# Sparse-attention encoder step: memory-branch pieces tied to a softmax, a weight pair split on ScalarE, values' low halves on VectorE

## The chip, the cores and the metric

The kernel runs on one core of one Trainium2 chip. The metric is the device time of one execution in microseconds, the median of the runs; lower is better. The engines are named as in the profile: PE is TensorE (matmuls; PEld its weight loads), DVE is VectorE, ACT is ScalarE, POOL is GpSimd, and SP is the engine that issues the transfers (DMAs).

## The reference

One layer of a streaming encoder on 1024 prompt tokens and 64 sample tokens, width 1024. Three branches of the normalised input are mixed by sigmoid gates:

```python
def dsa_attend(qa, qi, wi, qpos, ka, va, ki, topk):          # branch a
    s = jax.nn.relu(jnp.einsum('bthd,bsd->bths', qi, ki))
    score = jnp.einsum('bths,bth->bts', s, wi)               # indexer
    ...
    _, sel = lax.top_k(score, topk)
    ...
    logits = jnp.einsum('bthgd,btjhd->bthgj', q, k_sel) * (HD_A ** -0.5)
    probs = jax.nn.softmax(logits, axis=-1)
    return jnp.einsum('bthgj,btjhd->bthgd', probs, v_sel)

def merge_and_ffn(x, a, b, m, gates, w_oa, w_ob, w_om, w_out, g_ffn, w_gate, w_up, w_down):
    ga, gb, gm = jnp.split(jax.nn.sigmoid(gates), N_BRANCH, axis=-1)
    mixed = ga * (a @ w_oa) + gb * (b @ w_ob) + gm * (m @ w_om)
    x = x + mixed @ w_out
    h = rmsnorm(x, g_ffn)
    return x + (jax.nn.silu(h @ w_gate) * (h @ w_up)) @ w_down
```

Branch a has 8 query heads on 2 key heads of 64; b is a pooling mixer; m is attention into 256 memory tokens. The kernel does not gather the chosen keys: it adds a score that holds a large penalty for keys that were not chosen.

## The kernel before

Everything is one function, `encoder_step`, on one core. Float32 products are made of float32r halves: a value is rounded to a high half, the rest is its low half, and `matmul3` multiplies high by high, low by high and high by low. So each weight block of 128x1024 costs a DMA into `raw`, a rounding `whi` (`round_hi`: POOL, or ACT where `third[0]` says so, line 95) and a subtraction `wlo` on DVE (`lo_of`, line 87). `whi` and `wlo` are rings of two buffers, so a rounding waits until the matmuls of the block two before it are done.

The Tile framework places the instructions: it reorders what is written by its own timeline, so the order on an engine is not that of the source. Each engine then runs its own list in order and waits on semaphores. `tc.issue_after(x)` makes the instructions under it that run on the engine of x stand behind x in that engine's list.

The stage in question is the attention of branch a, 668 to 868 us of the profile. The tokens are nine blocks (b = 0 to 7 of 128 prompt tokens, 8 the sample's 64), walked in the order 2, 7, 1, 6, 0, 8, 5, 4, 3; block b has 128(b+1) keys. Around this stage the steps are:

- `fill_gate`: sigmoid gates (a tanh, `fsg`, on ACT, line 244), stored through DMAs to `side_a`; the last one runs at the stage's start. The loads of values (`vf`) and queries (`q`) follow on SP.
- `split_values`: high halves of all values (`vb`) on ACT (L947), low halves on POOL (L948), eight of each.
- `queries_t(b)`: loads q, splits it (`split_queries`: high on ACT, L803, low on POOL, L804), transposes it on PE into `qT`.
- `softmax(b, kv)`: for four heads, logits on PE (L985, into the `tr` banks), score added and a minimum taken on DVE (as the maximum of the negated logits; "maximum" below) (`pr`, `mx`, L995, one pass), exponential on ACT (L997); then a reciprocal on DVE (L999) and four normalisations on POOL (L1001).
- `values(b, kv)`: by 128 keys, four transposes of `pr` on PE (L1014), split on ACT (`ph`, L1017) and DVE (`pl`, L87), and two matmuls into `acc` (L1021); at the end a sum of the two halves (`ot` or `a_held`, L1025 to 1029). It runs one step behind its softmax.
- `halves_of` and `release`: branch a's result is split into `bh` (ACT, L1038) and `bl` (POOL or, for the last block, DVE, L1039). These replace branch m's, so the results of six blocks are held in `a_held` until the fills that read the old content are done.
- `fill_om(f, ci)`: a piece of the memory branch (row block f of eight, one of three column pieces `OCH`): 12 matmuls on PE (L123) into the single bank `fl`, a multiply with the gate on DVE (L639), an addition on POOL (L640), a DMA to `side_a` (L641). There are 24 such fills. They are PE work that depends on nothing in the attention, and they use 8 weight pairs: four for the first two column pieces, and four again for the third. "First", "second", "third", "fourth" pair mean these in order.
- `merge`: the same for branch a with `w_oa`; four of the merges are written right after the attention (`f` 0 to 3, first column piece, into `tr` banks) and read only blocks 0 to 2, which are released early. After them comes the row stage with the remaining merges (its first matmul here: L123 `mm`, 128x352).

The main loop runs softmax(b, kv), one fill (or two, late), then values of the step before.

Of the kernel before, what the change touches and what calls it, by code (L numbers as in the profile page):

```python
# [46 lines left out]
def encoder_step(ctx: ExitStack, tc: tile.TileContext, a: dict, o: list):  # L47
# [581 lines left out]

    def fill_om(f, ci, other=False):  # L630
        if (f // 2, ci == 2) not in om_w:
            om_w[f // 2, ci == 2] = wblock(a["w_om"][f:f + 2].rearrange("f p k j -> p f k j"), (2, 4, 128))
        ow = om_w[f // 2, ci == 2]
        c0, cn = OCH[ci]
        c1 = c0 + cn
        gt, pin = merge_bufs(side_m, f, c0, c1)
        ps = mm()[:, :cn] if other else fps(cn)
        matmul3(ps, [(ow[0][:, f % 2, k], ow[1][:, f % 2, k], bh[:, k, c0:c1], bl[:, k, c0:c1]) for k in range(4)])
        V.scalar_tensor_tensor(gt, gt, 1.0, ps, op0=OP.add, op1=OP.mult)  # L639
        G.tensor_tensor(pin, pin, gt, op=OP.add)  # L640
        SP.dma_start(side_a[f, 1, :, c0:c1], pin)  # L641
# [160 lines left out]
    def split_queries(qs, q, n, eng=V):  # L802
        A.copy(qs[:n, :, 0], q[:n])  # L803
        eng.tensor_tensor(qs[:n, :, 1], q[:n], qs[:n, :, 0].bitcast(F32), op=OP.subtract)  # L804
# [126 lines left out]
    HELD = (0, 1, 2, 6, 7, 8)  # L931
    a_held = []
    with tc.tile_pool(name="att", bufs=1, side="right") as ap_:
# [9 lines left out]
        def split_values():  # L943
            for b0, b1, n in ((0, 4, 128), (4, 8, 128), (8, 9, 128), (9, 10, 64)):
                for kv in range(2):
                    vs = vf[b0 // 8][:n, b0 % 8:b0 % 8 + b1 - b0, kv * HDA:(kv + 1) * HDA]
                    A.copy(vb[:n, b0:b1, kv, 0], vs)  # L947
                    G.tensor_tensor(vb[:n, b0:b1, kv, 1], vs, vb[:n, b0:b1, kv, 0].bitcast(F32), op=OP.subtract)  # L948

# [19 lines left out]
        def softmax(b, kv, qT):  # L969
            n, nk, k0 = TS[b][1], nkey[b], 0 if b < 8 else SEQ  # L970
            if True:
                probs = []
                sm = ap_.tile([128, 4], F32, name="sm", tag="sm", bufs=4)[:n]
                for g in ORDER:
# [20 lines left out]
                    V.tensor_tensor_reduce(as_view(pr, nk), bank_view(lg, nk)[:n], as_view(score[b][:n], nk),  # L995
                                           scale=1.0, scalar=3.4e38, op0=OP.add, op1=OP.min, accum_out=mx)
                    A.activation(pr, pr, AF.Exp, bias=mx, scale=-1.0, accum_out=sm[:, len(probs):len(probs) + 1])  # L997
# [6 lines left out]
        def values(b, kv, probs):  # L1004
# [3 lines left out]
            if True:  # L1008
                acc = psum[0].tile([128, 512], F32, name="acc", tag="acc", bufs=1)[:, :4 * n]
                nj = len(blocks)  # L1010
                for ji, (c, cn, vi) in enumerate(blocks):
                    pt = mm() if rest or ji % 3 != 2 else fps(512)
                    for i in range(4):
                        PE.transpose(pt[:cn, i * n:(i + 1) * n], probs[i][:, c:c + cn], ident[:n, :n])  # L1014
# [2 lines left out]
                    A.copy(ph, pt[:cn, :4 * n])  # L1017
                    lo_of(pl, pt[:cn, :4 * n], ph)
                    vv = vb[:cn, vi, kv].rearrange("p s d -> p (s d)")
                    for i, r in enumerate((ph, pl)):  # L1020
                        PE.matmul(acc, vv, r, start=ji == 0 and i == 0, stop=ji == nj - 1 and i == 1)  # L1021
# [15 lines left out]
        def halves_of(av, cs, t0, n, eng):  # L1037
            A.copy(aoh[:, cs, t0:t0 + n], av)  # L1038
            eng.tensor_tensor(aol[:, cs, t0:t0 + n], av, aoh[:, cs, t0:t0 + n].bitcast(F32), op=OP.subtract)  # L1039
# [10 lines left out]
        for b in BLOCKS:  # L1050
            qT = queries_t(b)
            for kv in range(2):
# [7 lines left out]
                for _ in range(1 if b in HELD else late_fills.pop(0)):  # L1060
                    fill_om(*rest.pop(0))
                if todo:
                    values(*todo)
# [4 lines left out]
        values(*todo)
        release(HELD[3:])

    def merge(f, c0, cn, gt, pin, ps):
# [4 lines left out]
        matmul3(ps, [(ow[0][:, f % 2, k], ow[1][:, f % 2, k], aoh[:, k, c0:c1], aol[:, k, c0:c1]) for k in range(4)])
        V.scalar_tensor_tensor(gt, gt, 1.0, ps, op0=OP.add, op1=OP.mult)
        V.tensor_tensor(pin, pin, gt, op=OP.add)

    oa_w, early_pin = {}, []  # L1080
    FIRST = [(f, 0) for f in range(0, KT, 2)]
    for f in range(4):
        gt, pin = merge_bufs(side_a, f, 0, ACH[0][1])
        merge(f, *ACH[0], gt, pin, tr()[:, :ACH[0][1]])
        early_pin.append(pin)
# [539 lines left out]
```

## Time and profile before

| | us |
|---|---|
| median of 3 runs (1716.28 to 1719.61) | 1718.47 |
| the profiled execution | 1719.66 |
| its span in the profile | 1717.9 |
| PE busy | 1687.7 (98%) |
| DVE busy | 1146.7 (67%) |
| ACT busy | 808.1 (47%) |
| POOL busy | 408.8 (24%) |

The mean granted TensorE clock is 0.996. Three quarters of the chain of work that ended last is in the matmuls of other stages; the stage 668 to 868 us is read by stretches. A stretch row has start and end, its length, the busy time of each engine with its number of instructions, the clock granted to TensorE, the share of the DMA engines and GB/s. In timeline rows the first number is the start, the second the duration; in brackets stands how long the engine was idle before and what ended that.

### The profile page before, as it was taken

What the parts mean: (1) busy time and instruction counts of PE and PEld (TensorE: products, weight loads), DVE (VectorE), ACT (ScalarE), POOL (GpSimd) and SP (SyncE); (2) the same over time, 40 slices, a digit from 0 to 9 for tenths busy, and PEclk for the clock granted to TensorE, in tenths of its full rate; (3) what the DMA queues carried; (4) which work ended last, traced back from release to release, by engine and by line L of the source; (5) the groups of instructions that cost most, each with busy time, mean ns of one, the idle gap of its engine ahead of it and who ended that gap; (6) DMA issues with size and microseconds to landing.
All of it is one profiled execution on the core that took longest, in us unless ns stands there. A gap on an engine that the chain in (4) does not pass through costs nothing.

```text
span 1717.9 us, 32353 instructions
## 1 busy us (share of the span) xinstructions
PE 1687.7 (98%) x11992; PEld 1639.2 (95%) x11992; DVE 1146.7 (67%) x2558; ACT 808.1 (47%) x1943; POOL 408.8 (24%) x479
## 2 busy tenths in 40 slices
PE   8999999999999998999999999999999999999999
PEld 7999999999999998997798999999999999999999
DVE  7566999999974342787773678557667666465543
ACT  5456677746633442568632443333334333353331
POOL 4200425355421122675303431001101000000000
PEclk9999999999999999999999999999999999999999
DMA  6121541223466325452176536443535443497661
GB/s 231 49 70 56 174 146 48 71 89 110 129 201 201 102 86 181 159 177 78 51 274 214 198 114 236 144 144 125 203 114 187 145 169 102 160 361 230 216 191 53
DMA packets 150654, 257.13 MB, mean 150 GB/s; under 512 B 17240, under 2 KB 95696, under 8 KB 150496
## 3 DMA queue, kind: packets, MB, share of 16 engines
q1 hardware_dynamic: 150496, 255.07, 45.4%
q8 instruction: 94, 1.54, 0.4%
q14 instruction: 64, 0.52, 0.1%
HBM read 175.73 MB, written 79.29 MB: 148 GB/s over the span
## 4 chain that ended last, share of the span: by engine, by line
PE 62%; DVE 4%; DMA 3%; issue 2%; ACT 1%; POOL 1%; SPq 0%; DVEq 0%; ACTq 0%; POOLq 0%
PE mm L1279 24%; PE mm L1506 12%; PE mm L123 11%; PE fl L123 8%; PE acc L1021 1%; PE tr L985 1%; DMA side_m<-fpt 1%; PE mm L1014 1%; DVE lo L87 1%; PE tr L123 0%; DMA raw<-s 0%; PE mm L674 0%; DVE pl L87 0%; DVE wlo L87 0%; DVE pr L995 0%
## 5 line engine op out<-in xcount | busy, mean ns | idle before, releaser
L1279 PE MATMUL mm<-hi,whi 128*128 128x288 f32 (+1 forms) x1120 | 323.1, 289 | 2.3 <-ACT whi L1271 2.3
L1279 PE MATMUL mm<-hi,wlo 128*128 128x288 f32 (+1 forms) x1120 | 323.7, 290 | 1.2 <-DVE wlo L87 1.0
L1279 PE MATMUL mm<-lo,whi 128*128 128x288 f32 (+1 forms) x1120 | 323.5, 289 | 0.0
L1279 PEld LDWEIGHTS mm<-hi,whi 128*128 128x128 f32 x1120 | 211.9, 189 | 3.0 <-ACT whi L1271 3.0
L1279 PEld LDWEIGHTS mm<-hi,wlo 128*128 128x128 f32 x1120 | 211.0, 189 | 1.7 <-DVE wlo L87 1.6
L1279 PEld LDWEIGHTS mm<-lo,whi 128*128 128x128 f32 x1120 | 211.8, 189 | 0.0
L123 PE MATMUL fl<-hh,whi 128*128 128x362 f32 (+1 forms) x576 | 190.0, 330 | 0.4 <-ACT hh L135 0.4
L123 PE MATMUL fl<-hl,whi 128*128 128x362 f32 (+1 forms) x576 | 189.7, 330 | 0.1
L123 PE MATMUL fl<-hh,wlo 128*128 128x362 f32 (+1 forms) x576 | 188.1, 330 | 0.0
L1506 PE MATMUL mm<-ul,wh 128*128 128x256 f32 (+1 forms) x600 | 171.7, 288 | 0.0
L1506 PE MATMUL mm<-uh,wh 128*128 128x256 f32 (+1 forms) x600 | 171.4, 289 | 0.1
L1506 PE MATMUL mm<-uh,wl 128*128 128x256 f32 (+1 forms) x600 | 170.4, 288 | 0.0
L854 ACT ACTIVATE junk_a<-score,cand_a,sgn_a 128x512 f16<-128x512 f32 (+2 forms) x93 | 95.5, 1027 | 42.4 <-DVE cand_a L871 30.8
L1506 PEld LDWEIGHTS mm<-uh,wh 128*128 128x128 f32 x600 | 112.5, 188 | 0.5 <-ACT wh L1496 0.3
L1506 PEld LDWEIGHTS mm<-ul,wh 128*128 128x128 f32 x600 | 112.8, 188 | 0.0
L1506 PEld LDWEIGHTS mm<-uh,wl 128*128 128x128 f32 x600 | 112.3, 188 | 0.0
L123 PEld LDWEIGHTS fl<-hh,whi 128*128 128x128 f32 x576 | 108.2, 188 | 1.7 <-ACT hh L135 0.6
L123 PEld LDWEIGHTS fl<-hl,whi 128*128 128x128 f32 x576 | 108.3, 188 | 0.9 <-DVE hl L87 0.4
L123 PEld LDWEIGHTS fl<-hh,wlo 128*128 128x128 f32 x576 | 108.0, 188 | 0.6
L87 DVE TENSOR_TENSOR wlo<-raw,whi 128x512 fp32r<-128x512 f32 (+1 forms) x64 | 66.1, 1047 | 61.6 <-ACT whi L1271 37.9
L87 DVE TENSOR_TENSOR wl<-raw,wh 128x512 fp32r<-128x512 f32 x75 | 51.7, 689 | 70.2 <-ACT wh L1496 70.2
L857 DVE TENSOR_SCALAR_CACHE_REDUCE junk_v<-score,cand_v 64x192 f16<-64x192 f32 (+1 forms) x124 | 93.9, 757 | 2.6
(431 smaller groups left out, 4597.1 us busy)
## 6 DMA issues: line engine op xcount, KB each, us to landing
uf<-u SPq DMA_DIRECT2D x75, 272.0 KB, 4.4
raw<-in_w_up_dram SPq DMA_DIRECT2D x26, 512.0 KB, 4.5
fraw<-in_w_gates_dram SPq DMA_DIRECT2D x23, 512.0 KB, 3.7
fr<-in_w_gate_dram SPq DMA_DIRECT2D x22, 512.0 KB, 3.7
dr<-in_w_down_dram SPq DMA_DIRECT2D x22, 512.0 KB, 5.7
s<-dr SPq DMA_DIRECT2D x22, 512.0 KB, 3.0
raw<-s SPq DMA_DIRECT2D x44, 256.0 KB, 4.0
raw<-in_w_down_dram SPq DMA_DIRECT2D x33, 256.0 KB, 3.7
```

The source lines that it names most:

```text
L87: return V.tensor_tensor(lo, src, hi.bitcast(F32), op=OP.subtract)
L123: PE.matmul(ps, l, r, start=i == 0, stop=i == len(prods) - 1)
L854: A.activation(junk[:n, :nk], sc, AF.Sign, bias=bj, scale=1.0 if scale is None else scale[:n, j:j + 1], accum_out=sj)
L857: V.tensor_scalar(junk[:n, :nk], sc, bj, None, op0=OP.is_ge, op1=OP.add, accum_out=sj)
L985: PE.matmul(lg[:n, i * 512:i * 512 + cn], qT[:, h, :n], kT[:, kv, s, k0 + c:k0 + c + cn], start=s == 0, stop=s == 1)
L1014: PE.transpose(pt[:cn, i * n:(i + 1) * n], probs[i][:, c:c + cn], ident[:n, :n])
L1021: PE.matmul(acc, vv, r, start=ji == 0 and i == 0, stop=ji == nj - 1 and i == 1)
L1279: PE.matmul(dst[i], l, r, start=start and j == 0, stop=stop and j == 11, skip_group_check=True)
L1506: PE.matmul(acc[f, i], l[:, fs], r[:, cs], start=start and j == 0, stop=stop and j == 2, skip_group_check=True)
```

## The change

- The second pair of memory weights is written right behind the first fill with `third[0] = 2`, so its rounding goes to ACT.
- Every fill in the main loop is written under `issue_after` of the last L995 instruction of that step's softmax. That instruction runs on DVE, so the tie holds the fill's multiply on DVE (L639), and nothing on PE or POOL.
- The values' low halves go from POOL to DVE.
- The high halves of the queries from the second block on, and those of the results that POOL splits, go from ACT to POOL.
- The four early merges are tied on PE: the first behind the last `acc` matmul of the last step but one, the second behind the last transpose of the last step, the third and fourth behind its last `acc` matmul.

```diff
+    def om_weights(f, ci):
         if (f // 2, ci == 2) not in om_w:
+            f -= f % 2
             om_w[f // 2, ci == 2] = wblock(a["w_om"][f:f + 2].rearrange("f p k j -> p f k j"), (2, 4, 128))
-        ow = om_w[f // 2, ci == 2]
+        return om_w[f // 2, ci == 2]
+
+    def fill_om(f, ci, other=False, after=None):
+        ow = om_weights(f, ci)
...
-        matmul3(ps, [(ow[0][:, f % 2, k], ow[1][:, f % 2, k], bh[:, k, c0:c1], bl[:, k, c0:c1]) for k in range(4)])
-        V.scalar_tensor_tensor(gt, gt, 1.0, ps, op0=OP.add, op1=OP.mult)
-        G.tensor_tensor(pin, pin, gt, op=OP.add)
+        with tc.issue_after(after) if after else nullcontext():
+            matmul3(ps, [(ow[0][:, f % 2, k], ow[1][:, f % 2, k], bh[:, k, c0:c1], bl[:, k, c0:c1]) for k in range(4)])
+            V.scalar_tensor_tensor(gt, gt, 1.0, ps, op0=OP.add, op1=OP.mult)
+            G.tensor_tensor(pin, pin, gt, op=OP.add)
...
-    for _ in range(1):
-        fill_om(*rest.pop(0))
+    fill_om(*rest.pop(0))
+    third[0] = 2
+    om_weights(2, 1)
+    third[0] = 0
...
     def split_queries(qs, q, n, eng=V):
-        A.copy(qs[:n, :, 0], q[:n])
+        if eng is V:
+            A.copy(qs[:n, :, 0], q[:n])
+        else:
+            G.tensor_scalar(qs[:n, :, 0], q[:n], 1.0, 1.0, op0=OP.mult, op1=OP.mult)
...
                     A.copy(vb[:n, b0:b1, kv, 0], vs)
-                    G.tensor_tensor(vb[:n, b0:b1, kv, 1], vs, vb[:n, b0:b1, kv, 0].bitcast(F32), op=OP.subtract)
+                    lo_of(vb[:n, b0:b1, kv, 1], vs, vb[:n, b0:b1, kv, 0])
...
-                    V.tensor_tensor_reduce(as_view(pr, nk), bank_view(lg, nk)[:n], as_view(score[b][:n], nk),
+                    last_mx[:] = [V.tensor_tensor_reduce(as_view(pr, nk), bank_view(lg, nk)[:n], as_view(score[b][:n], nk),
...
         def halves_of(av, cs, t0, n, eng):
-            A.copy(aoh[:, cs, t0:t0 + n], av)
+            if eng is V:
+                A.copy(aoh[:, cs, t0:t0 + n], av)
+            else:
+                G.tensor_scalar(aoh[:, cs, t0:t0 + n], av, 1.0, 1.0, op0=OP.mult, op1=OP.mult)
...
-                    fill_om(*rest.pop(0))
+                    fill_om(*rest.pop(0), after=last_mx[0])
...
+        ties = last_acc[:]
         values(*todo)
+        ties += last_tr + last_acc + last_acc
         release(HELD[3:])
...
-    for f in range(4):
+    for f, ins in enumerate(ties):
         gt, pin = merge_bufs(side_a, f, 0, ACH[0][1])
-        merge(f, *ACH[0], gt, pin, tr()[:, :ACH[0][1]])
+        merge(f, *ACH[0], gt, pin, tr()[:, :ACH[0][1]], ins)
```

`last_tr` and `last_acc` are set in `values` in the same way as `last_mx`, and `merge` puts its matmuls under `issue_after` of the instruction given.

What stands in a row on DVE at the start of the stage, before (`wlo_8964` is the third pair's low half; `tr` holds the logits of block 2, `score2` its scores):

```order
L639 SCALAR_TENSOR_TENSOR gt_8430<-gt_8430,fl_8432 128x384
L639 SCALAR_TENSOR_TENSOR gt_8448<-gt_8448,mm_8450 128x384
L639 SCALAR_TENSOR_TENSOR gt_8466<-gt_8466,mm_8468 128x384
L995 ISA pr_8488,mx_8489<-tr_8485,score2_94 128x384
L995 ISA mx_8489 128x1
L995 ISA pr_8488,mx_8494<-tr_8485,score2_94 128x384
L995 ISA mx_8494 128x1
L995 ISA pr_8500,mx_8501<-tr_8497,score2_94 128x384
L995 ISA mx_8501 128x1
L87 TENSOR_TENSOR wlo_8964<-raw_8962,whi_8963 128x1024
L995 ISA pr_8500,mx_8506<-tr_8497,score2_94 128x384
```

And now, at the same place:

```order
L87 TENSOR_TENSOR vb_8427<-vf_8431,vb_8427 128x4x64 x3
L644 SCALAR_TENSOR_TENSOR gt_8454<-gt_8454,mm_8456 128x384
L87 TENSOR_TENSOR vb_8427<-vf_8431,vb_8427 128x4x64
L87 TENSOR_TENSOR vb_8427<-vf_8432,vb_8427 128x64 x2
L87 TENSOR_TENSOR vb_8427<-vf_8432,vb_8427 64x64 x2
L644 SCALAR_TENSOR_TENSOR gt_8472<-gt_8472,mm_8474 128x384
L1005 ISA pr_8494,mx_8495<-tr_8491,score2_94 128x384
L1005 ISA mx_8495 128x1
L87 TENSOR_TENSOR wlo_8964<-raw_8962,whi_8963 128x1024
L1005 ISA pr_8494,mx_8500<-tr_8491,score2_94 128x384
```

The values' low halves came in among the multiplies, and the third pair's `wlo` moved from behind the third maximum to behind the first.

POOL from the first block to the first normalisation, before (`qs_8650` the queries of block 7, `whi_8963` the third pair):

```order
L640 TENSOR_TENSOR gt_7674<-gt_7674 128x384
L948 TENSOR_TENSOR vb_8421<-vf_8425,vb_8421 128x4x64 x4
L640 TENSOR_TENSOR gt_8430<-gt_8430 128x384
L948 TENSOR_TENSOR vb_8421<-vf_8426,vb_8421 128x64 x2
L948 TENSOR_TENSOR vb_8421<-vf_8426,vb_8421 64x64 x2
L804 TENSOR_TENSOR qs_8650<-q_8646,qs_8650 128x8x64
L640 TENSOR_TENSOR gt_8448<-gt_8448 128x384
L97 TENSOR_SCALAR whi_8963<-raw_8962 128x1024
L640 TENSOR_TENSOR gt_8466<-gt_8466 128x384
```

And now, on to the fourth pair, `whi_9448`, and the first normalisation of block 7 (`pr_8670`):

```order
L813 TENSOR_SCALAR qs_8650<-q_8646 128x8x64
L645 TENSOR_TENSOR gt_8454<-gt_8454 128x384
L814 TENSOR_TENSOR qs_8650<-q_8646,qs_8650 128x8x64
L97 TENSOR_SCALAR whi_8963<-raw_8962 128x1024
...
L645 TENSOR_TENSOR gt_8706<-gt_8706 128x384
L97 TENSOR_SCALAR whi_9448<-raw_9447 128x1024
L1011 TENSOR_SCALAR pr_8670<-pr_8670,sm_8664 128x1024
```

The values left the list, and a high half of the queries, which needs their DMA, stands ahead of the third rounding.

PE at the end of the attention, before (`acc` the last values, `mm_10766` the row stage's first merge):

```order
L1021 MATMUL acc_10577<-ph_10605,vb_8421 128x512
L1021 MATMUL acc_10577<-pl_10606,vb_8421 128x512
L1021 MATMUL acc_10577<-ph_10616,vb_8421 128x512
L1021 MATMUL acc_10577<-pl_10617,vb_8421 128x512
L123 MATMUL mm_10766<-bh_1711,whi_10640 128x352
L123 MATMUL mm_10766<-bl_1712,whi_10640 128x352
```

And now (`tr_10661` the second early merge, `tr_10678` the third):

```order
L123 MATMUL tr_10661<-bl_1712,whi_10640 128x384
L1031 MATMUL acc_10577<-pl_10595,vb_8427 128x512
L1031 MATMUL acc_10577<-ph_10605,vb_8427 128x512
L123 MATMUL tr_10661<-bh_1711,wlo_10641 128x384
L1031 MATMUL acc_10577<-pl_10606,vb_8427 128x512
L1031 MATMUL acc_10577<-ph_10616,vb_8427 128x512
L1031 MATMUL acc_10577<-pl_10617,vb_8427 128x512
L123 MATMUL tr_10678<-bh_1711,whi_10680 128x384
```

The third and fourth merges, 24 matmuls, now follow the last values, ahead of the row stage.

More of the change, by code (lines that the diff above doesn't have):

```diff
@@ L628, in merge_bufs @@
         return t[:, 0], t[:, 1]
-    def fill_om(f, ci, other=False):
+    def om_weights(f, ci):
         if (f // 2, ci == 2) not in om_w:
+            f -= f % 2
             om_w[f // 2, ci == 2] = wblock(a["w_om"][f:f + 2].rearrange("f p k j -> p f k j"), (2, 4, 128))
-        ow = om_w[f // 2, ci == 2]
+        return om_w[f // 2, ci == 2]
+    def fill_om(f, ci, other=False, after=None):
+        ow = om_weights(f, ci)
         c0, cn = OCH[ci]
@@ L931, in encoder_step @@
     HELD = (0, 1, 2, 6, 7, 8)
-    a_held = []
+    a_held, last_mx, last_tr, last_acc = [], [], [], []
     with tc.tile_pool(name="att", bufs=1, side="right") as ap_:
@@ L994, in softmax @@
                     mx = ap_.tile([128, 1], F32, name="mx", tag="mx", bufs=4)[:n]
-                    V.tensor_tensor_reduce(as_view(pr, nk), bank_view(lg, nk)[:n], as_view(score[b][:n], nk),
-                                           scale=1.0, scalar=3.4e38, op0=OP.add, op1=OP.min, accum_out=mx)
+                    last_mx[:] = [V.tensor_tensor_reduce(as_view(pr, nk), bank_view(lg, nk)[:n], as_view(score[b][:n], nk),
+                                           scale=1.0, scalar=3.4e38, op0=OP.add, op1=OP.min, accum_out=mx).ins]
                     A.activation(pr, pr, AF.Exp, bias=mx, scale=-1.0, accum_out=sm[:, len(probs):len(probs) + 1])
@@ L1013, in values @@
                     for i in range(4):
-                        PE.transpose(pt[:cn, i * n:(i + 1) * n], probs[i][:, c:c + cn], ident[:n, :n])
+                        last_tr[:] = [PE.transpose(pt[:cn, i * n:(i + 1) * n], probs[i][:, c:c + cn], ident[:n, :n]).ins]
                     ph = ap_.tile([128, 512], F32R, name="ph", tag="ph", bufs=3)[:cn, :4 * n]
@@ L1020, in values @@
                     for i, r in enumerate((ph, pl)):
-                        PE.matmul(acc, vv, r, start=ji == 0 and i == 0, stop=ji == nj - 1 and i == 1)
+                        last_acc[:] = [PE.matmul(acc, vv, r, start=ji == 0 and i == 0, stop=ji == nj - 1 and i == 1).ins]
                 ot = ap_.tile([128, 256], F32, name="ot", tag="ot", bufs=1)[:, :2 * n].rearrange("p (c t) -> p c t", c=2)
@@ L1067, in encoder_step, with merge @@
                 todo = (b, kv, probs)
+        ties = last_acc[:]
         values(*todo)
+        ties += last_tr + last_acc + last_acc
         release(HELD[3:])
-    def merge(f, c0, cn, gt, pin, ps):
+    def merge(f, c0, cn, gt, pin, ps, after=None):
         c1 = c0 + cn
@@ L1075, in merge @@
         ow = oa_w[f // 2]
-        matmul3(ps, [(ow[0][:, f % 2, k], ow[1][:, f % 2, k], aoh[:, k, c0:c1], aol[:, k, c0:c1]) for k in range(4)])
+        with tc.issue_after(after) if after else nullcontext():
+            matmul3(ps, [(ow[0][:, f % 2, k], ow[1][:, f % 2, k], aoh[:, k, c0:c1], aol[:, k, c0:c1]) for k in range(4)])
         V.scalar_tensor_tensor(gt, gt, 1.0, ps, op0=OP.add, op1=OP.mult)
```

## The prediction

> **What bounds the kernel now.** I read the cores' spans, then busy time by stretches, the waits of PE in each stretch, and the timeline around the two longest. PE is busy 1687.74 of the 1717.9 us, so 30.2 us are idle. The attention stage, all the change touches, lies between 668 and 868 us (columns: us; busy PE, weight loads, DVE, ACT, POOL; granted TensorE clock, DMA share, GB/s):
>
> ```profile
> 668.00:697.00 29.00, 24.11 (x132) 22.90 (x131) 11.78 (x28) 11.82 (x32) 17.32 (x24) 0.88 0.74 251
> 697.00:777.00 80.00, 79.53 (x498) 73.02 (x497) 65.53 (x135) 51.11 (x112) 53.03 (x59) 1.00 0.54 164
> 777.00:836.00 59.00, 54.43 (x320) 41.98 (x319) 46.61 (x118) 50.79 (x120) 31.51 (x42) 0.97 0.13 41
> ...
> 850.00:868.00 18.00, 13.81 (x71) 11.22 (x70) 12.05 (x24) 9.45 (x21) 0.73 (x1) 0.91 0.33 108
> ...
> sum 1718.00, PE 1687.74 PEld 1639.18 DVE 1146.73 ACT 808.09 POOL 408.79; mean PE 210.97 PEld 204.90 DVE 143.34 ACT 101.01 POOL 51.10
> ```
>
> Three stretches leave PE waiting: 29.00−24.11 = 4.89 us at the start, 0.47+4.57 in the middle, 4.19 in the tail, 14.1 in all. The clock is lowered in the same three: 29×0.12 = 3.5, 59×0.03 = 1.8 and 18×0.09 = 1.6 us, together 6.9. So 21 us is the most that the change can win. Two-microsecond stretches show where the clock falls:
>
> ```profile
> 686.00:688.00 2.00, 0.86 (x3) 0.87 (x4) 2.00 (x7) 0.89 (x3) 0.00 (x0) 0.50 0.43 154
> ...
> 802.00:804.00 2.00, 1.52 (x14) 1.09 (x13) 1.78 (x5) 1.94 (x6) 2.00 (x3) 1.00 0.02 4
> 804.00:806.00 2.00, 1.53 (x7) 1.13 (x7) 0.43 (x2) 2.00 (x5) 1.50 (x2) 0.83 0.00 0
> 806.00:808.00 2.00, 2.00 (x9) 1.84 (x8) 0.50 (x1) 1.98 (x6) 1.29 (x1) 0.50 0.04 8
> ...
> 864.00:866.00 2.00, 2.00 (x8) 2.00 (x8) 1.84 (x4) 1.37 (x4) 0.00 (x0) 0.50 0.94 301
> ```
>
> The drop at 806 us follows two stretches with only 0.48+0.47 us idle: here about 1 us of scattered waiting was enough. PE's waits by what ended them (line waited for: us, times, longest), for the start, the middle and the tail:
>
> ```profile
> PE tr L985 <- DVE mx L995: 4.1, 2, 3.4
> PE fl L123 <- ACT qT L817: 0.8, 1, 0.8
> ...
> PE tr L985 <- DVE mx L995: 1.3, 4, 0.4
> PE mm L1014 <- DVE pl L87: 1.0, 3, 0.5
> ...
> PE mm L123 <- DVE ot L1029: 1.8, 1, 1.8
> PE acc L1021 <- ACT ph L1017: 1.4, 2, 1.0
> ```
>
> In the middle PE waits in small pieces on DVE; at the start and in the tail single waits of 3.4 and 1.8 us lead.
>
> **The start (weights on ACT, values' lows on DVE, queries' highs on POOL).** These rows show the 3.4 us: POOL works through the values' lows and the first queries, then rounds the third weight pair; DVE's `wlo` waits for it, and the next logits' maximum stands behind `wlo`:
>
> ```profile
> 668.72 1.06 POOL L97 TENSOR_SCALAR whi<-raw 128x1024 fp32r<-128x1024 f32 x1 [10.94 <-PE fl L123]
> 668.88 0.47 ACT L244 ACTIVATE fsg<-fl 128x362 f32<-128x362 f32 x1 [3.58 <-PE fl L123]
> 676.45 2.82 POOL L948 TENSOR_TENSOR vb<-vf,vb 128x256 fp32r<-128x256 f32 x4 [3.88 <-ACT vb L947]
> 680.20 1.15 POOL L948 TENSOR_TENSOR vb<-vf,vb 128x64 fp32r<-128x64 f32 x4
> 678.85 0.62 ACT L803 CAST qs<-q 128x512 fp32r<-128x512 f32 x1 [0.97 <-DMA q<-q_a]
> ...
> 683.53 1.03 POOL L97 TENSOR_SCALAR whi<-raw 128x1024 fp32r<-128x1024 f32 x1
> 684.59 2.01 DVE L87 TENSOR_TENSOR wlo<-raw,whi 128x1024 fp32r<-128x1024 f32 x1 [1.54 <-POOL whi L97]
> 687.13 1.65 PE L985 MATMUL tr<-kT,qT 128*128 128x384 f32 x4 [3.40 <-DVE mx L995]
> ```
>
> POOL loses 2.82+1.15 = 4.0 us of lows. It gains the first queries' high half, and that one must wait for q, ahead of everything behind it in POOL's queue, the third rounding too. q was there at 678.85. The rounding of pair two on ACT saves POOL nothing that mattered (10.94 us idle ahead of it), but now stands ahead of the last `fsg`, whose DMA the loads of vf and q follow: ACT's same-sized rounding, below, takes 1.05 us, so q comes between 678.85 (nothing passed on) and 679.9. From there POOL does: high half, priced by the 732 ns row below, 0.73; one addition, 1.01; low half, 1.43; rounding, 1.05: it ends at 683.1 to 684.1 instead of 684.56. `wlo`, 1.87, ends at 685.0 to 686.0 instead of 686.5.
>
> ```profile
> L1001 POOL TENSOR_SCALAR pr<-pr,sm 128x512 f32<-128x512 f32 x8 | 5.7, 732 | 6.0 <-DVE sm L999 6.0
> L640 POOL TENSOR_TENSOR gt<-gt 128x384 f32<-128x384 f32 x16 | 16.1, 1008 | 18.4 <-issue 11.3 <-DVE gt L639 3.7 <-DVE sm L999 2.6
> L804 POOL TENSOR_TENSOR qs<-q,qs 128x512 fp32r<-128x512 f32 x7 | 10.0, 1426 | 3.3 <-ACT qs L803 3.3
> L97 POOL TENSOR_SCALAR whi<-raw 128x1024 fp32r<-128x1024 f32 x9 | 9.4, 1048 | 18.3 <-PE fl L123 16.9 <-DMA gt<-side_m 1.4
> L1039 DVE TENSOR_TENSOR bl<-ot,bh 128x256 fp32r<-128x256 f32 x2 | 0.8, 418 | 0.5 <-ACT bh L1038 0.5
> L87 DVE TENSOR_TENSOR wlo<-raw,whi 128x1024 fp32r<-128x1024 f32 x9 | 16.8, 1866 | 13.4 <-POOL whi L97 13.4
> L87 DVE TENSOR_TENSOR wlo<-fraw,whi x27: 1204/1218/2048, 16.8 to 642.2; 128x1024 fp32r<-128x1024 f32 x27
> L95 ACT CAST whi<-raw x17: 1031/1049/1052, 872.2 to 1040.4; 128x1024 fp32r<-128x1024 f32 x17
> ```
>
> But the order now lets only one maximum, not three, past before `wlo`, so PE runs dry sooner: I take 1 us won, the middle of the 0.5 to 1.5 that `wlo` gains, and leave the clock's 3.5 where they are. Ends: if PE has to wait only 2.3 us and the clock stays up, 0.8+4.1+3.5 = 8.4 becomes 3.1, 5.3 won; if it waits 5.5 us and the clock drops as before, 9.8, 1.4 lost. The lows on DVE, four at 418 ns and four smaller, below 0.42, add up to 3.4 us at most and end while PE does a fill; should that cover go, they come on top of the same wait.
>
> Here a rule bears on it. The Trainium skill ("SBUF — State Buffer", the shared port pair) says that a DVE instruction with two SBUF inputs and a GpSimd one that reads SBUF shut each other out for a whole instruction. The rows agree: `wlo` takes 1866 ns in this stage against 1218 where POOL is quiet; by that ratio the lows would cost 0.64 each and the sum not change, as they would still fit in 3.4 us.
>
> **The middle (a fill behind its softmax).** The fills' multiplies (L639) by stretch, and three rows of the second:
>
> ```profile
> 668.00:697.00 29.00, 3.31 (x6) 0.88 0.74 251
> 697.00:777.00 80.00, 8.91 (x18) 1.00 0.54 164
> ...
> 679.38 0.33 PE L123 MATMUL fl<-bh,whi 128*128 128x384 f32 x1
> ...
> 681.29 0.33 PE L123 MATMUL fl<-bh,wlo 128*128 128x384 f32 x1
> 702.27 1.05 POOL L97 TENSOR_SCALAR whi<-raw 128x1024 fp32r<-128x1024 f32 x1 [2.66 <-PE fl L123]
> ...
> 710.76 4.43 POOL L1001 TENSOR_SCALAR pr<-pr,sm 128x1024 f32<-128x1024 f32 x4
> ```
>
> All 24 fills are over when the third stretch, the one that waits, begins. The first two rows are the first and last of the 12 matmuls of one fill: 2.07 us at 0.17 each after the first.
>
> Only the multiply on DVE gets the new tie, behind the last maximum; since there is one `fl` bank, PE's next fill then waits for it. With one fill for each block and half, some eight fills, 16 us of PE, move from the second stretch to the third: PE 64 us against DVE 65.5−8×0.55−4×1.87 = 53.6 there, and 71 against 58.5 later. So 4.57+1.8 of waiting and clock should shrink to about 1. The price: the normalisation of block 7's first half (4.43 us) stands behind the fourth rounding, which waits for its buffer, freed by a fill that is now later, and behind a maximum-bound reciprocal. PE had two fills (4.1 us) there and has one (2.07); 4.43+1.05−2.07 leaves 3.4, less some 0.4 of logits in between: 3.0 us new. Won: 0.47+4.57+1.8−1.0−3.0 = 2.8. Ends: no new wait, 6 won; two such waits (6.0) with a lowered window of 1.7 us each, 9.4 against 6.8, 2.6 lost.
>
> The queries' and halves' highs on POOL (six more queries, 0.73 each; five halves as wide) add 8 us to POOL, which loses the lows and has 27 us idle in the second and 27 in the third stretch: nothing, unless they push a normalisation, which the lower end holds. ACT loses 0.62 and 0.62 a piece and was waiting anyhow: nothing.
>
> **The tail (merges tied on PE).** The last early merge, and the first matmul of the row stage:
>
> ```profile
> 849.48 0.34 PE L123 MATMUL tr<-bh,wlo 128*128 128x384 f32 x1
> ...
> 862.83 0.40 PE L123 MATMUL mm<-bh,whi 128*128 128x352 f32 x1 [1.82 <-DVE ot L1029]
> ```
>
> After 849.8 the values run bare for 11 us and PE waits 4.19−1.82 = 2.4 us in pieces; then it waits 1.8 us, and the clock falls. Now merges two and three, 24 matmuls at 0.174 = 4.2 us, stand in exactly that gap: 1.8+1.6 = 3.4 won. Two of the merges no longer cover the groups of values ahead of 849 us. By the bare stretch (2.4 us over eight groups) a group costs 0.3, and I count two more bare ones: 0.6 lost, 2.8 won. Ends: 5.8, all of that stretch; 0.8, if the bare groups lower the clock (1.6) and cost 1 more.
>
> Sum: 1.0+2.8+2.8 = 6.6, from the profiled execution's 1719.66 us to 1713.1. That execution lies 1.2 above the median of the runs shown, 1718.47; in medians 1711.9, say 1712.
>
> **Rivals.** *The waits only move.* Blocks 7 and 6 get fewer fills and the bare tail groups wait; the middle is zero and the tail 0.8: 1718.47−1.8 = 1716.7, 1715 to 1721. For it speaks that the normalisations of these two blocks, 4.43 us at a time, are the longest, and DVE is busy 65.5 of 80 us in the stretch that now loses its fills. Against it, that stretch had only 0.47 us of waiting.
>
> *Slower, by POOL's order.* Each of the four roundings in the middle waits for the buffer of a paced fill with normalisations behind it. If PE waits 3 us in each, and each lowers one window by 1.7, 18.8 us stand against the 6.8 that the middle loses today and 3.8 won at its ends: 8 slower, 1726. It decides from 10.6/4 = 2.7 us a pair, clock included, and tells in a measurement from 3.5. For it: POOL's 18.3 us idle ahead of `whi`, 16.9 of them on PE. Against: the order puts most of them behind the normalisation they could hold.
>
> *Much faster.* q at 678.85 passes, PE waits 2.3 at the start and the clock stays: 5.3+5+4 = 14.3, 1704 to 1709.
> The Trainium skill ("TensorE: Matmul & The Clock Gate", What's actually happening) has the clock fall only after an idle window of about 3.4 us. The trace speaks against: at 806 us it fell after 1 us idle. As a mechanism of this kernel (no lowering after waits under 3.4 us) it would take the 3.5 us of clock that I leave at the start out of the sum: 1708.5.
>
> **How the numbers follow.** The forecast has 0.48, with its own range 1709 to 1715; the waits that move 0.24; slower 0.14; much faster 0.14, of which 0.05 by the clock alone. A measurement of this kernel tells 0.2%, 3.4 us, from no change: faster is below 1715.0 (0.48+0.14), slower above 1721.9. The range 1705 to 1721.5 leaves out about 0.05 below and 0.14 above.
>
> **What would show it.** Right: the third `wlo` ends by 686, fills appear up to the last blocks, PE near full from 777 to 850 us, no lowered clock near 806, and merge matmuls between the last values and the row stage without a gap. Wrong: PE waiting over 3 us for `mx` or the normalised `pr` in the first 40 us, roundings with normalisations held behind them, or a lowered clock at new places.

## The result and the profile after

| | median us (runs) | ratio to before, 95% interval |
|---|---|---|
| before | 1718.47 (1715.44 to 1720.22) | |
| changed | 1738.12 (1734.48 to 1741.82) | 1.0116 [1.0104, 1.0128] |

The changed kernel is 1.16% slower, some 20 us; the forecast was 1712. Its profiled execution took 1738.09 us.

The same stretches of the stage as before, and what follows (us; busy PE, weight loads, DVE, ACT, POOL; clock, DMA share, GB/s):

```profile
668.00:697.00 29.00, 22.42 (x118) 20.88 (x117) 12.55 (x27) 7.84 (x22) 11.63 (x12) 0.88 0.72 237
697.00:777.00 80.00, 74.16 (x441) 63.16 (x438) 57.51 (x139) 54.53 (x123) 46.83 (x57) 1.00 0.32 99
777.00:836.00 59.00, 51.64 (x319) 45.71 (x317) 44.93 (x92) 35.06 (x81) 33.73 (x39) 0.91 0.29 90
836.00:860.00 24.00, 20.02 (x112) 15.73 (x112) 19.24 (x43) 15.53 (x37) 18.92 (x25) 0.98 0.43 143
860.00:886.00 26.00, 23.53 (x126) 19.94 (x125) 17.15 (x34) 10.44 (x23) 5.55 (x9) 0.95 0.43 144
```

PE's idle time went from 4.89 to 6.6 us at the start, from 0.47 to 5.8 in the second stretch, which had been full, and from 4.57 to 7.4 in the third, where the clock is now 0.91. All that is lost lies in the attention stage: from the first fill's first matmul to the row stage's first one it took 862.83−668.63 = 194.2 us before and takes 883.52−671.02 = 212.5 now. Of these 18.3 us, 12.1 are idle time of PE (26.2 against 14.1) and 6.2 longer busy time of PE (186.3 against 180.1), at a mean granted clock of 0.95 instead of 0.97. This "stage length" is used below; in it the upstream part, whose end varies by some 5 us between the profiles, drops out.

The largest waits of PE, for 668 to 697, 777 to 800 and 836 to 860 us (line waited for: us, times, longest):

```profile
PE tr L995 <- DVE mx L1005: 5.8, 3, 4.4
...
PE mm L1024 <- DVE pl L87: 5.8, 1, 5.8
...
PE mm L1024 <- DVE sm L1009: 1.9, 1, 1.9
```

The single wait of 5.8 us is new. This is DVE's and POOL's timeline at that place, DVE first (start, duration):

```profile
782.22 0.35 DVE L1005 CUSTOM_DVE_ANT_0 pr<-tr,score 64x192 f32<-64x192 f32 x1
782.49 6.13 DVE L87 TENSOR_TENSOR wlo<-raw,whi 128x1024 fp32r<-128x1024 f32 x1
788.54 0.68 DVE L87 TENSOR_TENSOR pl<-mm,ph 128x512 fp32r<-128x512 f32 x1
...
781.05 1.05 POOL L97 TENSOR_SCALAR whi<-raw 128x1024 fp32r<-128x1024 f32 x1
782.07 1.21 POOL L1051 TENSOR_SCALAR bh<-a_held 128x512 fp32r<-128x512 f32 x2
783.23 1.28 POOL L1052 TENSOR_TENSOR bl<-a_held,bh 128x512 fp32r<-128x512 f32 x1
784.47 0.63 POOL L813 TENSOR_SCALAR qs<-q 128x512 fp32r<-128x512 f32 x1
785.05 1.27 POOL L1052 TENSOR_TENSOR bl<-a_held,bh 128x512 fp32r<-128x512 f32 x1
786.27 1.27 POOL L814 TENSOR_TENSOR qs<-q,qs 128x512 fp32r<-128x512 f32 x1
```

A weight pair's subtraction that takes 1.21 to 2.30 us elsewhere in this stage takes 6.13, while POOL works without a gap: POOL's chain ends at 787.54, the subtraction 1.08 us later. PE waits for the `pl` behind it:

```profile
789.28 1.12 PE L1024 MATMUL mm<-ident,pr 128*128 128x128 f32 x4 [5.80 <-DVE pl L87]
```

and then runs at half clock (the stretch behind it):

```profile
790.00:794.00 4.00, 4.00 (x13) 3.60 (x12) 3.03 (x8) 1.03 (x3) 2.63 (x5) 0.50 0.47 172
```

At the start the first maximum comes at 688.3 us (679.8 before); 2.4 us of that is the later start of the whole stage (671.02 against 668.63). SP and ACT before, then SP, ACT and DVE now, show the rest:

```profile
671.35 0.37 SPq L939 DMA_DIRECT2D vf<-v_a  x1
676.58 1.07 SPq L112 DMA_DIRECT2D raw<-in_w_om_dram  x1
675.96 1.92 ACT L947 CAST vb<-vf 128x256 fp32r<-128x256 f32 x8 [3.67 <-DMA vf<-in_cache_a_v_dram]
```

```profile
673.44 0.38 SPq L112 DMA_DIRECT2D raw<-in_w_om_dram  x1
674.51 0.37 SPq L949 DMA_DIRECT2D vf<-v_a  x1
...
681.56 1.91 ACT L957 CAST vb<-vf 128x256 fp32r<-128x256 f32 x8 [6.89 <-DMA vf<-v_a]
...
682.00 1.09 DVE L87 TENSOR_TENSOR vb<-vf,vb 128x256 fp32r<-128x256 f32 x3 [4.27 <-ACT vb L957]
683.48 3.97 DVE L87 TENSOR_TENSOR vb<-vf,vb 128x256 fp32r<-128x256 f32 x5
687.38 0.54 DVE L644 SCALAR_TENSOR_TENSOR gt<-gt,mm 128x384 f32<-128x384 f32 x1
687.84 0.54 DVE L1005 CUSTOM_DVE_ANT_0 pr<-tr,score 128x384 f32<-128x384 f32 x1
```

The early second pair brought the third pair's load ahead of the values' load; the values were split from 681.56 instead of 675.96 (10.5 us after the first fill began instead of 7.3), and their eight subtractions, 5.1 us on DVE beside POOL, stand ahead of the first maximum.

### The profile page after: what moved, and what is told of

Read it like the earlier page. It is cut to its first block, busy times and chain, and to the rows that moved or that the text cites. A ratio compares the mean times of both kernels' runs of the same rounds, so it can differ in the third digit from the quotient of the medians.

```text
span 1736.0 us, 32336 instructions
## 1 busy us (share of the span) xinstructions
PE 1692.9 (98%) x11992; PEld 1641.7 (95%) x11992; DVE 1152.8 (66%) x2566; ACT 802.1 (46%) x1926; POOL 416.1 (24%) x488
## 4 chain that ended last, share of the span: by engine, by line
PE 86%; DVE 6%; issue 3%; DMA 2%; ACT 2%; POOL 1%; SPq 0%; DVEq 0%; POOLq 0%; ACTq 0%
PE mm L1295 23%; PE mm L123 23%; PE fl L123 18%; PE mm L1522 13%; PE tr L995 2%; PE acc L1031 2%; PE mm L1024 1%; PE mm L380 1%; DVE wlo L87 1%; DVE lo L87 1%; DVE pl L87 1%; PE mm L679 0%; DVE pr L1005 0%; DMA vf<-v_a 0%; DVE fr L1249 0%
```

## The experiments

Two theories. **Port**: a DVE instruction that has only SBUF operands stands still as long as POOL works on SBUF without a gap; the change put longer POOL chains beside such instructions and took away the PE work that used to cover them. (The runs bear out that DVE is held, but not always as long as this; the last section has the count.) **Order**: PE's waits come from what stands in line (paced fills, values' lows, the late load), and the long subtraction is a by-product. All kernels are the changed one or the one before with the edits shown. The medians are of four to eleven executions and each ratio is to the kernel before on the same chip; the stage length is that of the one profiled execution:

| kernel | median us | ratio to before | stage length, us |
|---|---|---|---|
| changed, again | 1737.7 | 1.0108 [1.0093, 1.0124] | 214.5 |
| changed, fills untied (u_fill) | 1717.7 | 1.0002 [0.9992, 1.0011] | 194.0 |
| changed, results' highs back on ACT (u_hhi) | 1730.2 | 1.0075 [1.0052, 1.0097] | 206.5 |
| changed, values' lows back on POOL (u_vals) | 1732.3 | 1.0087 [1.0066, 1.0109] | 208.6 |
| changed, no early pair (u_om) | 1731.0 | 1.0079 [1.0060, 1.0097] | 207.6 |
| changed, held results off POOL (x_rel) | 1730.3 | 1.0062 [1.0047, 1.0077] | 204.2 |
| changed, one pair's low half from one operand, another pair than meant (x_one) | 1733.6 | 1.0082 [1.0065, 1.0099] | 213.0 |
| changed, the same for the pair meant (x_one2) | 1734.4 | 1.0090 [1.0076, 1.0104] | 208.2 |
| changed, three undone (u3) | 1726.1 | 1.0040 [1.0025, 1.0054] | 203.5 |
| before + ties of fills (p_fill) | 1727.2 | 1.0045 [1.0029, 1.0061] | 198.9 |
| before + ties + highs on POOL (f_hi) | 1730.5 | 1.0066 [1.0051, 1.0081] | 205.8 |
| before + ties + lows on DVE + early pair (f_vo) | 1732.7 | 1.0082 [1.0065, 1.0098] | 207.5 |
| before + ties of merges (p_merge) | 1717.6 | 0.9987 [0.9977, 0.9998] | 192.4 |
| p_merge + early loads (c_kt) | 1723.5 | 1.0025 [1.0016, 1.0035] | 198.9 |
| p_merge + roundings on ACT (c_allact) | 1715.9 | 0.9983 [0.9972, 0.9993] | 191.2 |

**One part undone at a time.** Fills untied:

```diff
-                    fill_om(*rest.pop(0), after=last_mx[0])
+                    fill_om(*rest.pop(0))
```

> The changed kernel without the ties of the fills to the maxima; it is the part that moves most instructions. If the paced fills cost the middle (waits of 5.1 us between 700 and 780 us against 0.5 before, and the 5.8 us wait at 783), it gains 8 to 14 us: 1724 to 1730. If the middle's loss is the port's, met by chance at one place, it gains only what the small waits were, less what the third stretch then loses: 1734 to 1738.

All 20 us came back. PE is full again from 700 to 780 us, and of the other parts together nothing is left to see in the time:

```profile
700.00:780.00 80.00, 80.00 (x509) 74.01 (x508) 63.12 (x136) 48.89 (x109) 60.10 (x68) 1.00 0.55 169
780.00:800.00 20.00, 16.12 (x106) 13.31 (x105) 16.91 (x42) 14.34 (x40) 11.10 (x18) 1.00 0.25 85
```

That is more than either theory expected, so the ties are needed for the rest to cost anything. The trace still shows single costs. PE is idle for 5.9 us up to 697 us, and at 779.74 a subtraction of 3.11 us stands beside POOL, with a wait of PE of 2.87 us behind it:

```profile
779.74 3.11 DVE L87 TENSOR_TENSOR wlo<-raw,whi 128x1024 fp32r<-128x1024 f32 x1
...
780.50 1.26 POOL L1052 TENSOR_TENSOR bl<-a_held,bh 128x512 fp32r<-128x512 f32 x1
781.73 1.58 POOL L813 TENSOR_SCALAR qs<-q 128x512 fp32r<-128x512 f32 x1
```

Against them stand a clock that stays at 1.00 from 693 us on and the tied merges. Results' highs back on ACT:

```diff
         def halves_of(av, cs, t0, n, eng):
-            if eng is V: ... else: G.tensor_scalar(aoh[:, cs, t0:t0 + n], av, 1.0, 1.0, ...)
+            A.copy(aoh[:, cs, t0:t0 + n], av)
```

> The changed kernel, but the high halves of the attention's results go back from POOL to ACT. Port theory (a DVE subtraction with both inputs in SBUF stands still while POOL works back to back on SBUF): the POOL chain around 782 us loses 1.2 us and gets a gap, the weights' subtraction there falls from 6.13 us to under 3, PE's wait behind it from 5.8 to under 2.5, and the lowered clock after it goes: 1729 to 1733 us against 1738. Order theory (waits come only from what stands in line): the order hardly differs, so 1737 to 1739.

The total came as the port theory said, but the subtraction only to 3.77 us; PE still waits 3.4 us behind it, and the clock is still lowered after it (0.86 from 784 to 796 us). Its rows (DVE first):

```profile
779.01 3.77 DVE L87 TENSOR_TENSOR wlo<-raw,whi 128x1024 fp32r<-128x1024 f32 x1
...
778.61 2.51 POOL L1049 TENSOR_TENSOR bl<-a_held,bh 128x512 fp32r<-128x512 f32 x2
781.10 0.61 POOL L813 TENSOR_SCALAR qs<-q 128x512 fp32r<-128x512 f32 x1
781.79 2.12 POOL L814 TENSOR_TENSOR qs<-q,qs 128x512 fp32r<-128x512 f32 x1
```

POOL has a gap of 0.08 us at 781.71; the subtraction ends 1.07 us after it, and this time POOL's next instruction is the one that is held (2.12 us against 1.27).

Values' lows back on POOL, and no early second pair:

```diff
-                    lo_of(vb[:n, b0:b1, kv, 1], vs, vb[:n, b0:b1, kv, 0])
+                    G.tensor_tensor(vb[:n, b0:b1, kv, 1], vs, vb[:n, b0:b1, kv, 0].bitcast(F32), op=OP.subtract)
```
```diff
-    third[0] = 2
-    om_weights(2, 1)
-    third[0] = 0
```

> The changed kernel, but the values' low halves go back to POOL. If their place on DVE ahead of the first maximum is the cost of the start (first maximum at 687.8 us, 8.5 us later than before), the first maximum comes at about 681, but POOL's rounding of the third pair then ends 4 us later, about 690: PE's waits at the start change from 5.8 to 4-5 us, 1736 to 1738. If the port is the cost (their 5.5 us on DVE are stretched by POOL), the same work on POOL takes 4.0 us, and DVE is free: 1733 to 1736.

> The changed kernel without the early second pair on ACT: its rounding is back on POOL, and its subtraction and the next pair's DMA lose their early places. If the late load of the values (issued at 674.5 us, behind the third pair's DMA and the late last tanh) is what holds the start, the values arrive 2 to 3 us earlier and PE's waits at the start shrink from 5.8 to about 3 us: 1734 to 1736. If the queue of work on DVE and POOL is what holds it, nothing changes: 1737 to 1739.

Each gained more than expected (3.9 and 4.9 us of stage, 5.8 and 7.1 in the medians). With u_om the values' subtractions start at 675.9 us, so the late load is the early pair's doing; the 6.13 us subtraction stood in both.

**The port by itself.** First the low half of one weight pair from one SBUF operand:

```diff
-        lo_of(lo, raw, hi)
+        if one:
+            V.tensor_scalar(lo, hi.bitcast(F32), 2.0 ** -13, 1.0, op0=OP.mult, op1=OP.mult)
+        else:
+            lo_of(lo, raw, hi)
```

> The changed kernel; only the low half of one weight pair (memory branch, rows 0 and 1, third column piece, the 6.13 us subtraction) is made on DVE from one input, a multiple of the high half, so that it reads one SBUF operand and not two; the true low half of that pair is left out. Order on all engines as in the changed kernel. Port theory in its narrow form (two SBUF inputs against POOL): it takes 0.6 to 1.3 us though POOL works on beside it, PE's 5.8 us wait falls under 1.5, no lowered clock at 790: 7 to 10 us won, 1728 to 1731. If any DVE instruction on SBUF is held off while POOL is at it: 5 to 6 us again, 1738.

I had picked the wrong pair: the edit fell on the one at 755.9 us (0.68 us there), and the subtraction of 6.13 us stood as before. The kernel so serves as another run of the changed one: stage 213.0 us, median 1733.6. That is 4 us below the changed kernel's own median, with an edit that touches 0.5 us of DVE's work; so differences of a few us between kernels run on different chips carry little by themselves. The second try took the pair meant (`one` for rows 2 and 3), beside the changed kernel on the same chip:

> The changed kernel once more, for the comparison with the next one on the same chip and for its spread: 1733 to 1739 us, a 6 us subtraction at about 780 us and PE's 5.8 us wait behind it in this profile too. If that event were chance, it would be gone or elsewhere.

> The changed kernel; the low half of the memory pair of rows 2 and 3, third column piece, is made on DVE from one SBUF input (a multiple of the high half) instead of two; the true low half of that pair is left out. This is the subtraction that took 6.13 us. Port theory in its narrow form (two SBUF inputs against POOL): 0.7 us here as in x_one's other pair, PE's 5.8 us wait under 1, and the lowered clock after it gone: 5 to 9 us less than the changed kernel on this chip. If any DVE instruction on SBUF stands still while POOL is at it: 5 to 6 us again and no change.

```profile
780.35 4.38 DVE L115 TENSOR_SCALAR wlo<-whi 128x1024 fp32r<-128x1024 f32 x1
784.65 0.68 DVE L87 TENSOR_TENSOR pl<-mm,ph 128x512 fp32r<-128x512 f32 x1
...
782.90 1.27 POOL L1055 TENSOR_TENSOR bl<-a_held,bh 128x512 fp32r<-128x512 f32 x1
787.03 1.01 POOL L648 TENSOR_TENSOR gt<-gt 128x384 f32<-128x384 f32 x1 [2.85 <-DVE gt L647]
```

The narrow form falls: with one SBUF operand it is held as well, until POOL's chain ends at 784.17, and then takes its own 0.6 us. PE waits 4.0 us behind it, and the lowered clock after it is still there (0.84 from 786 to 796 us). The event is no chance: 6.13 us in the second run of the changed kernel too, and the same six POOL instructions held it in all six traces that have them in this order. That run's 1737.7 against 1734.4 here: 3.3 us, less than the 5 to 9 expected; the intervals of the two ratios overlap.

Then the held results taken off POOL:

```diff
-                halves_of(held_of(b, slice(0, 4)), slice(0, 4), *TS[b], G)
+                halves_of(held_of(b, slice(0, 4)), slice(0, 4), *TS[b], V)
```

> The changed kernel, with both halves of the held results (release) off POOL: highs on ACT, lows on DVE, four of the chain's seven instructions at 782 us. Port theory: the chain is over by 784, the subtraction takes at most 2.5 us, PE's wait falls from 5.8 to 2 or less (some of it for the lows now on DVE, 0.7 us each): 6 to 10 won, 1728 to 1732. Order theory: DVE has more to do ahead of what PE waits for, 1738 to 1742.

DVE's and POOL's timeline at the place, and the stretch around it:

```profile
783.18 1.21 DVE L87 TENSOR_TENSOR wlo<-raw,whi 128x1024 fp32r<-128x1024 f32 x1
...
783.52 1.34 POOL L813 TENSOR_SCALAR qs<-q 128x512 fp32r<-128x512 f32 x1 [1.97 <-issue]
```

```profile
780.00:800.00 20.00, 17.54 (x115) 15.85 (x114) 16.12 (x36) 13.86 (x31) 9.32 (x13) 1.00 0.28 83
```

POOL is idle when the subtraction starts, and it takes 1.21 us; now POOL's next instruction is the one that is held (1.34 us against 0.63). PE is idle for 2.5 us in the stretch, 5.8 in the changed kernel, the lowered clock at 790 is gone, and the stage is 8.3 us shorter although DVE has more to do: the order theory is wrong on this place.

**Parts added to the kernel before.** The ties of the fills alone, then with the highs on POOL, then with the two parts that touch the start:

> The kernel before with one part alone: the fills tied to the last maximum of their softmax. If the ties by themselves cost (PE loses its filler from 697 to 777 us and a weight pair's subtraction meets the results' halves on POOL), 1727 to 1738. If they cost only together with the highs that were moved to POOL and lengthen its chain (6.13 us subtraction), 1717 to 1724. By my prediction of the middle (2.8 won) it would be 1715 to 1717.

> The kernel before with two parts: the tied fills and the high halves (queries and results) on POOL. If the highs lengthen the POOL chains that hold DVE's subtractions (6.13 us at 782 us in the changed kernel, 3.52 with the ties alone), the long subtraction is back, with a lowered clock behind it: 5 to 8 us above the ties alone (1727), 1732 to 1735. If it takes more than these two parts: 1726 to 1729.

> The kernel before with three parts: the tied fills, the values' low halves on DVE and the early second pair on ACT. If these cost at the start what undoing them gave (3.9 and 4.9 us of stage), the first maximum stands behind the values' lows as in the changed kernel and PE idles about 7 us up to 700 us against 4.6: 3 to 6 us above the ties alone, 1730 to 1733. If the start was long in any case: 1726 to 1729.

The ties alone cost 7.7 us, against all of my expectations but the first. Where it happens in the kernel with the ties alone (DVE, POOL, PE; then the stretches):

```profile
775.76 3.52 DVE L87 TENSOR_TENSOR wlo<-raw,whi 128x1024 fp32r<-128x1024 f32 x1 [0.48 <-POOL whi L97]
779.48 0.54 DVE L644 SCALAR_TENSOR_TENSOR gt<-gt,fl 128x384 f32<-128x384 f32 x1
...
775.70 2.50 POOL L1043 TENSOR_TENSOR bl<-a_held,bh 128x512 fp32r<-128x512 f32 x2
...
780.07 0.44 PE L123 MATMUL fl<-bh,whi 128*128 128x320 f32 x1 [3.04 <-DVE gt L644]
```

```profile
700.00:780.00 80.00, 74.73 (x457) 64.83 (x455) 60.33 (x145) 59.66 (x138) 47.69 (x58) 1.00 0.33 100
780.00:800.00 20.00, 19.43 (x115) 18.24 (x115) 15.41 (x34) 12.06 (x26) 9.72 (x12) 0.91 0.29 83
```

A held subtraction (POOL's chain ends at 778.20, it ends 1.08 us later) delays the fill's multiply, `fl` stays taken, and PE waits 3.0 us at the next fill; then the clock falls. PE idles 5.3 us from 700 to 780, these 3.0 among them. The fills did move: 84 of the 204 matmuls into `fl` that stood between 697 and 777 us now come later. In the kernel before the long subtractions were there too (3.50 us at 725.68), but PE had untied fills beside them.

With the highs the subtraction grows to 6.15 us again (778.57) and a lowered clock follows; f_hi came out 1.5 us below its band. With the lows and the early pair the first maximum ends at 686.7 us, behind `vb` as in the changed kernel, and PE idles 7.15 us up to 700 us (4.6 with the ties alone). Against before the parts make 0.45% (ties), 0.21% more (highs), 0.37% more (start), −0.13% (merges): 0.90%, of the 1.08 to 1.16% measured. The rest is within the intervals of these differences, which are about 0.2% each, or interplay; the runs do not tell which. The reverse, three parts undone:

> The changed kernel with three things undone: the held results' halves off POOL (as x_rel), the values' lows back on POOL, the early pair dropped; left are ties, queries' highs and tied merges. If the costs of port and start are separate, they add to x_rel's 8 and about 4 more: 1724 to 1727, the level of the ties alone. If only one of them shows at a time: 1729 to 1732.

It lies at the ties' level, as expected if the costs of port and start add. That they add is not shown: the stage of its one profiled execution, the slowest of five, is only 0.7 us shorter than x_rel's, and the single gains of u_vals, u_om and x_rel (5.8, 7.1 and 7.8 us in the medians) sum to 20.7 us where u3 gained 12. One thing more can be read here. No subtraction of the stage takes over 2.01 us in u3, and still it is 0.40% slower than before. So the ties cost without a long hold too: PE's waits are of 1.5 us at most from 700 us on, but they come in groups, and the clock is at half for 6.8 us twice, from 814 and from 848 us.

**The tail, and two new versions.** The tied merges alone:

```diff
-        merge(f, *ACH[0], gt, pin, tr()[:, :ACH[0][1]])
+        merge(f, *ACH[0], gt, pin, tr()[:, :ACH[0][1]], ins)
```

> The kernel before with one part alone: the four early merges tied on PE. By the prediction (24 matmuls in the 1.8 us gap before the row stage, no lowered clock after it, 0.6 lost ahead) 2.8 won: 1714 to 1716. If the groups of values that lose the merges wait as much as the gap was, 1717 to 1720.

0.13% faster, some 2.2 us, [0.3, 4.0]; the row stage's first matmul waits 1.06 us instead of 1.82, and the clock stays at 1.00 from 850 to 890 us, where it had been 0.96. Then two attempts on top of it:

```diff
+        om_weights(2, 1)
+        third[0] = 2
+        om_weights(4, 1)
+        raw3 = raw_ld[0]
+        third[0] = 0
         late_fills = [2, 2, 1, 1, 1, 1]
...
-                with tc.issue_after(ld.ins):
+                with tc.issue_after(raw3):
                     load_keys(384, 768)
```

> A new version: the kernel before with the tied merges (p_merge); the second and third memory pairs are written ahead of the main loop, the third one's rounding goes to ACT, and the loads of the later keys (1.7 MB) go out behind an early weight load instead of behind the second queries' load, so that they no longer fill the DMA queues at the start of the stage. If the third pair's load (6.5 us under way, landing at 683.1 us in the profile before) is what held the 3.4 us wait at the start, PE's waits there fall from 4.9 to 1-2 us and the clock stays up: 4 to 7 us less than before, 1712 to 1715. If POOL's and DVE's queue held it, about as p_merge: 1716 to 1718.

It came to 1723.5 us, 1.0025 [1.0016, 1.0035]: a miss. The early loads did bring the third `wlo` to 681.8 us (684.6 before), but PE then waited 4.4 us for `fl`, and at 777.01 us a subtraction of 4.32 us met POOL's chain and cost PE another 4.3. The second, all roundings of memory pairs on ACT:

```diff
+            third[0] = 2
             om_w[f // 2, ci == 2] = wblock(a["w_om"][f:f + 2].rearrange("f p k j -> p f k j"), (2, 4, 128))
+            third[0] = 0
```

> A new version: the kernel before with the tied merges (p_merge), all roundings of memory pairs on ACT, so that POOL has nine instructions fewer on the port and no normalisation waits behind a rounding. The subtractions of weights then take 1.22 us more often (nine took 16.8 us before, 5.8 above that). If DVE's held subtractions cost PE waits in the middle: 1 to 3 us below p_merge, 1714 to 1717. If ACT, 86% busy from 777 to 836 us, delays what PE waits for: 1718 to 1722.

1715.9 us, faster than both kernels; nine subtractions now take 1.21 to 1.86 us, none above, and the start's waits fell to 3.2 us:

```profile
668.00:700.00 32.00, 28.78 (x156) 26.09 (x155) 15.48 (x36) 16.96 (x40) 18.89 (x25) 0.95 0.73 244
```

Against p_merge it is not told apart.

## Why the prediction was wrong

Of the 6.6 us forecast only the tail came. The step that decides is the middle: the ties of the fills were counted as 2.8 us won, and they lose 7.7 alone; without them nothing is lost.

- **The start, 1.0 won.** Failed in two steps. I let the values' lows "end while PE does a fill", with 3.4 us at most; they took 5.1 us, their split began 5.6 us later (3.2 counted from the stage's start), and so they stood in front of the first maximum. And of the early pair I counted the late tanh (it came about 1 us later), but not that it moves the third pair's load past the values' on SP. f_vo puts the two at some 6 us (0.37%) with the fills tied; with the fills untied (u_fill) they cost nothing that the time shows.
- **The middle, 2.8 won.** The new waits in block 7 came in the size given: 1.4 us for POOL's normalisation and 1.4 in two others, against 3.0. But the shrinking of the third stretch's waits did not come: with the ties alone PE idles 3.7 us from 780 to 850 us against 4.6 before, so 15 us of moved fills saved 0.9 us, while the second stretch lost 4.8. DVE's load of 0.84, from which I concluded that little would wait there, is a mean; what counts is the wait behind one instruction when PE has nothing else: 3 to 6 us where a subtraction is held, and up to 1.5 us at a time where none is (u3).
- **The highs on POOL, counted at nothing "unless they push a normalisation".** They pushed nothing to be seen: PE's wait for the normalisation is 1.0 us with them (f_hi) and without (p_fill). But they lengthened POOL's chain behind the rounding near 776 us from two instructions to six, and the subtraction beside it from 3.52 to 6.15 us. I had the rule in hand: the Trainium skill ("SBUF — State Buffer", SBUF: two separate sides) says that a DVE instruction with two SBUF inputs and a GpSimd one that reads SBUF shut each other out for a whole instruction. The traces agree that they do, but here DVE was at times shut out for several POOL instructions (six for the 6.13 us). I priced it by the mean of 1866 ns and for the values' lows alone. The trace of before showed the size that one such case can have, behind that mean: POOL's chain ends at 728.10, the subtraction at 729.18, 1.08 us later.

```profile
725.68 3.50 DVE L87 TENSOR_TENSOR wlo<-raw,whi 128x1024 fp32r<-128x1024 f32 x1
...
724.87 1.29 POOL L804 TENSOR_TENSOR qs<-q,qs 128x512 fp32r<-128x512 f32 x1
726.12 1.98 POOL L640 TENSOR_TENSOR gt<-gt 128x384 f32<-128x384 f32 x2
```

- **The tail, 2.8 won.** Right in mechanism and about in size: 2.2 us, [0.3, 4.0].
- **The rivals.** "Slower, by POOL's order" had the sign and the engine, not the mechanism: it is not mainly normalisations that wait behind a rounding (1.4 us), but DVE that waits for POOL. None of the cases reached 1738, and the range had no term for the port.
- **The clock.** By the mean granted clock of the stage (0.95 against 0.97 before) the lowered clock took about 10.6 us of it against 5.8. The rule of the Trainium skill that the prediction quotes ("TensorE: Matmul & The Clock Gate", What's actually happening) asks for an idle window of about 3.4 us before the clock falls. The traces do not agree: in u3 the clock fell at 814.2 us with no wait of PE over 1.02 us in the 10 us before, and in u_fill a wait of 2.87 us lowered nothing. What decides it stays open.

## What to carry to other kernels

Before work is moved to GpSimd, list the VectorE instructions with only SBUF operands that will run beside it, and look at the longest of them, not the mean: most waited for one GpSimd instruction, but a chain without gaps can stop one to the chain's end. Filler for TensorE that is tied to another engine's progress is not there when that engine is held, so tie it only where its absence has a price that was looked up.

## What the runs showed of the hardware

In the seventeen traces, 92 subtractions of a weight pair in the stage (668 to 862 us) took 1.3 us or more, against 1.21 alone. Every one of them ended 1.07 to 1.09 us after the end of a POOL instruction. 77 waited for one POOL instruction, 15 for two to six (2.5 to 6.15 us for the same 1.21 us of work). A gap in POOL's chain is not needed: in 58 of the 92 POOL's next instruction followed without one, and it was that instruction which then took about 1 us longer.

So a chain without gaps can hold a subtraction to its end, as at 782 us, but need not. In the changed kernel one came in between the two `bl` of a chain, the second of which took 2.25 us instead of 1.27:

```profile
855.69 2.30 DVE L87 TENSOR_TENSOR wlo<-raw,whi 128x1024 fp32r<-128x1024 f32 x1
...
855.64 3.48 POOL L1052 TENSOR_TENSOR bl<-a_held,bh 128x512 fp32r<-128x512 f32 x2
```

In the second run of the changed kernel the same instructions in the same order, the subtraction again 0.05 us behind the first `bl`, held it for four POOL instructions: it took 5.01 us (from 854.87), and PE waited 4.65 us behind it instead of 1.93; the stage lengths of the two runs differ by 2.0 us. What decides when DVE is let in is not shown.

A TENSOR_SCALAR with one SBUF operand was held too (4.38 us, 0.68 in the other pair). `pl`, which reads one operand from PSUM, was not: none of 1190 in the stages of these traces took over 0.70 us, though 455 ran beside POOL for nine tenths of their time or more. In the same chain, two took 1.38 us together:

```profile
859.46 1.38 DVE L87 TENSOR_TENSOR pl<-mm,ph 128x512 fp32r<-128x512 f32 x2
...
859.90 0.73 POOL L1052 TENSOR_TENSOR bl<-a_held,bh 128x256 fp32r<-128x256 f32 x1
860.61 2.70 POOL L1011 TENSOR_SCALAR pr<-pr,sm 128x512 f32<-128x512 f32 x4
```
